# A two-block hybrid layer stack: first block's projections moved ahead, as block products through DRAM

## The chip, the cores and the metric

One Trainium2 chip, one core. The metric is device microseconds (us) from the start to the end of one execution, the median of several runs.

## What is computed

Two transformer-like blocks follow each other on 1024 tokens of width 1024; only the first is changed. It puts 16 learned tokens in front (1040 in all), normalises, and multiplies by one wide matrix `w_in`. The columns of that product feed two mixers, whose gated outputs are summed, projected and added to the input.

```python
u = rmsnorm(h, norm_pre);  proj = u @ w_in
z_ssd, xbc, dt_raw, z_att, q, k, v, f_raw, g_raw = split(proj)
# SSD mixer: 32 heads of 64 channels in 4 groups, chunks of 128 tokens
xs, bm, cm = split(silu(causal_depthwise_conv(xbc)))
dt = softplus(dt_raw + dt_bias);  a_cs = cumsum(dt * a)          # inside a chunk
decay = exp(where(causal, a_cs[l] - a_cs[s], -inf))
y = (C B^T * decay) @ (xs*dt)  +  exp(a_cs) * (C @ h_in)         # h_in: state carried from chunk to chunk
y_ssd = gated_group_rmsnorm(y + d_skip * xs, z_ssd)
# forgetting attention: 16 heads of 64, causal
logit[t, s] = q_t . k_s / 8 + sum_{s<j<=t} log sigmoid(f_j)
y_att = (softmax(logit) @ v) * silu(z_att)
merged = sigmoid(g) * (y_ssd @ w_proj_ssd), sigmoid(g') * (y_att @ w_proj_att), added
x1 = h + rmsnorm(merged @ w_out)
```

The second block (differential and dilated attention, gated embedding) follows on `x1`.

## The kernel before

Everything is channel-major, in strips of 128 channels by all tokens. A projection of a strip (`project`) is a sum over eight row blocks of the input; each float32 product is done as three matmuls of rounded parts (`mm3`, lines 111 to 114: high with high, low with high, high with low), over pieces of at most 512 tokens, one PSUM bank each. The weights of a strip come by DMA on SP's queue, ScalarE (ACT) makes the high part, GpSimd (POOL) subtracts for the low part (`split_sb`, lines 117 to 121). The first block has 88 strips: 48 are needed for 1024 tokens (q, the gates za, zs and g) and 40 for 1040 (k, v and the 24 of the convolution's input `xbc`).

The order of work is written out by hand: generators yield after each piece with an estimate of TensorE's time, and `merge` interleaves two of them in a given ratio. Each engine runs its instructions in the order in which this code emits them.

- Attention goes head pair by head pair (eight), `fox_attend`: for each of eight query tiles, stage A makes the scores (lines 566 to 569), on VectorE (DVE) the sum with the forget gates and a running minimum (line 570), the exponential on ACT (line 573) and a small copy on POOL (line 576); stage B transposes (line 620) and evacuates (line 626); stage C multiplies by v (line 599). While a pair's tiles run, the projections of the next pair stand between them.
- The SSD goes group by group (four): first the group's six strips are projected and convolved (`ssd_project`), then eight chunks run (`ssd_chunks`), with the eight strips of zs and g between their steps. A chunk's step prepares the next one (`prep`: decayed exponentials on lines 714 to 722) and then does its own products (lines 747 and 750) and sums.

```python
            nx = {}
            if p < 7:
                merge(att, self.fox_project(p + 1, nx), 2.5, lead=2000.0)
...
            side = chain(z, zipped(self.gates(ms), rows))
            merge(self.ssd_chunks(g, st), side, 2.0 if g < 3 else 1.7)
```

Projected strips stay in SBUF until they are used; only the mixers' outputs and the gates go to DRAM. Then `merge_out` multiplies by the two output matrices, and the second block begins.

Of the kernel before, what the change touches and what calls it, by code (L numbers as in the profile page):

```python
# [22 lines left out]
SLOT = 1044  # L23
EPS = 1e-6
# [42 lines left out]
class Kern:  # L67
    def __init__(self, ctx, tc, t, out):
        self.tc, self.nc, self.t, self.out = tc, tc.nc, t, out
        self.big = ctx.enter_context(tc.tile_pool(name="big", bufs=41))  # L70
# [6 lines left out]
        self.halfs = None  # L77

# [5 lines left out]
    def half(self, name):  # L84
        """512 columns; in the tail from a pool of their own"""
# [4 lines left out]
    def psum(self, one, two):  # L90
        """the banks of PSUM from here on: single ones and pairs"""
# [40 lines left out]
    # weight strips, in the order in which they are used  # L132
# [63 lines left out]
    def consts(self):  # L196
# [16 lines left out]
        V.tensor_scalar(out=self.gbh, in0=self.pslot("gate_bias"), scalar1=0.5, scalar2=None, op0=ALU.mult)  # L213
        self.sb48 = cst.tile([48, 1], F32, name="sb48")
        V.tensor_tensor(out=self.sb48, in0=self.pslot("b48")[:48], in1=self.pslot("sgn")[:48], op=ALU.mult)

# [1 line left out]
    def rstd(self, out, ss, n):  # L218
        """1 / sqrt(ss / n + eps)"""
# [9 lines left out]
    def rsqrt(self, v, pool):  # L229
        """v [128, n] > 0 in place to 1/sqrt(v): a first guess from the exponent, three Newton steps"""  # L230
# [29 lines left out]
    def token_sums_T(self, t, n):  # L260
        """the sums by tokens: [128 tokens, block of 128, part, 32]"""
# [5 lines left out]
    def rows_out(self, v, n, dst):  # L267
        """v [128 tokens, n = (row, block of 128)]: rows of 1024 tokens in DRAM"""
# [22 lines left out]

    def prologue(self):
        nc, t = self.nc, self.t
        self.uh = [self.slot(f"uh{k}", F32R) for k in range(KD)]
        self.ul = [self.slot(f"ul{k}", F32R) for k in range(KD)]
        rows = [t["meta_tokens"]] + [t["x"][i * 128:(i + 1) * 128] for i in range(8)]
        ss = self.cst.tile([128, 9], F32, name="ss0")
        xs = []
        for i, r in enumerate(rows):
            p = r.shape[0]  # L300
            x = self.slot("x", w=D)
            nc.sync.dma_start(out=x[:p], in_=r)
            xs.append(x)
            if i == 0:
                self.const_loads()
            if i == 2:
                self._wload(0)
                self._wload(1)
        gain = self.pslot("norm_pre")
        for g, c0 in (((0, 1, 2), 0), ((3, 4, 5), 272), ((6, 7, 8), 656)):  # L310
            for i in g:
                p = rows[i].shape[0]
                j = self.slot("junk", w=D)
                nc.scalar.activation(out=j[:p], in_=xs[i][:p], func=AF.Square, accum_out=ss[:p, i:i + 1])
                self.rstd(ss[:p, i:i + 1], ss[:p, i:i + 1], D)
                nc.vector.tensor_scalar(out=xs[i][:p], in0=xs[i][:p], scalar1=ss[:p, i:i + 1], scalar2=None,
                                        op0=ALU.mult)
            yield
            if c0 == 0:
                self.consts()  # L320
            self.normed_T([xs[i][:rows[i].shape[0]] for i in g], gain, self.u1, c0)
            yield

# [1 line left out]
    def softplus(self, x):  # L325
        """x [128, 9, n] in place to max(x, 0) + log(1 + exp(-|x|)), the logarithm by the series of artanh"""
# [16 lines left out]
    def dt_f(self):  # L343
        nc, cst = self.nc, self.cst
        raw = self.slot("dtf")
        sgn = self.pslot("sgn")

        def consume(ps, c0, c1):
            nc.scalar.activation(out=raw[:48, c0:c1], in_=ps, func=AF.Identity, scale=sgn[:48], bias=self.sb48)

        yield from self.project("w48", self.u1, PIECES_P, consume, m=48)
# [10 lines left out]
        V = nc.vector  # L362
        self.softplus(sp[:, :, 32:48])
        yield 3000
        # cumulative log forget gates (negated: csp), as rows
# [27 lines left out]
        nc.sync.dma_start(out=self.d_csp, in_=row[:16, :L])  # L393
        self.softplus(sp[:, :, 0:32])
# [1407 lines left out]
```

## Time and profile before

| | |
|---|---|
| median of three runs | 2735.22 us (2734.06 to 2739.91) |
| the profiled execution's own span | 2737.4 us |
| busy: TensorE (PE), DVE, ACT, POOL | 2670.8, 1377.0, 1171.9, 685.0 us |
| granted TensorE clock, mean | 0.994 |
| first block, up to the first matmul of `merge_out` | 0 to 1421 us |
| attention's pairs | 79 to about 682 us |
| SSD's groups | about 660 to 1401 us |
| `merge_out`, w_out and the second block | 1421 to 2737 us |

The profile gives no separate run time for the profiled execution; its span lies 2.2 us (0.08%) above the median. "Busy" is the time in which an engine has an instruction under way; matmuls overlap each other, so TensorE's pace is read from the distance between starts and not from the duration of one.

### The profile page before, as it was taken

The page shows a single profiled execution, that of the slowest core. Times are in us where ns is not written, and L with a number is a line of the kernel's source. Part 1 is how long each engine was busy: PE and PEld are TensorE (multiplying, and loading weights), DVE is VectorE, ACT ScalarE, POOL GpSimd, SP SyncE. Part 2 cuts the span into 40 slices and gives each one's busy share as a digit, 9 for nine tenths or more (in the row PEclk, how much of TensorE's full clock was granted, in tenths as well). Part 3 has the DMA queues.
Part 4 walks back from the last instruction along what each step waited for, and adds up shares of the span by engine and source line. Part 5 has one row for each costly group of instructions (what it writes and reads, how often), then busy time and mean ns, then how long its engine had stood idle before and what let it go on. Part 6 is the DMA issues. An engine that isn't in the chain of part 4 may idle for free. (4 is left out here: it accounts for less than half of the span.)

```text
span 2737.4 us, 40266 instructions
## 1 busy us (share of the span) xinstructions
PE 2670.8 (98%) x15693; PEld 2264.5 (83%) x15693; DVE 1377.0 (50%) x2761; ACT 1171.9 (43%) x2080; POOL 685.0 (25%) x764
## 2 busy tenths in 40 slices
PE   8999999999999999999999999999999999998999
PEld 6888888889989989889887887877878877787887
DVE  5433222333474574664756777445644555446332
ACT  5444444454343443434432113445544554445331
POOL 1111111111244243342433334111111121114321
PEclk9999999999999999999999999999999999999999
DMA  3212222211123123122157654340222223324422
GB/s 124 65 57 78 71 78 78 78 47 47 70 83 118 47 85 116 49 84 108 62 186 253 215 185 161 108 130 26 85 62 78 79 79 97 98 72 138 166 67 70
DMA packets 85471, 266.98 MB, mean 98 GB/s; under 512 B 10880, under 2 KB 12032, under 8 KB 84256
## 3 DMA queue, kind: packets, MB, share of 16 engines
q1 hardware_dynamic: 85280, 264.40, 29.9%
q8 instruction: 123, 2.02, 0.3%
q14 instruction: 68, 0.56, 0.1%
HBM read 205.57 MB, written 33.49 MB: 87 GB/s over the span
## 5 line engine op out<-in xcount | busy, mean ns | idle before, releaser
L121 POOL TENSOR_TENSOR wlo<-wraw,whi 128x1024 fp32r<-128x1024 f32 (+2 forms) x168 | 374.3, 2231 | 1279.5 <-ACT whi L120 1242.6
L112 PE MATMUL bank<-uh,whi 128*128 128x512 f32 (+4 forms) x1752 | 628.4, 359 | 0.1
L114 PE MATMUL bank<-uh,wlo 128*128 128x512 f32 (+4 forms) x1752 | 619.7, 354 | 0.4 <-POOL wlo L121 0.4
L113 PE MATMUL bank<-ul,whi 128*128 128x512 f32 (+4 forms) x1752 | 619.5, 354 | 0.0
L112 PEld LDWEIGHTS bank<-uh,whi 128*128 128x128 f32 (+1 forms) x1752 | 328.9, 188 | 36.4 <-issue 3.5
L114 PEld LDWEIGHTS bank<-uh,wlo 128*128 128x128 f32 (+1 forms) x1752 | 328.6, 188 | 35.9 <-POOL wlo L121 0.9
L113 PEld LDWEIGHTS bank<-ul,whi 128*128 128x128 f32 (+1 forms) x1752 | 328.9, 188 | 32.2
L112 PE MATMUL bank<-u,whi 128*128 128x512 f32 x512 | 207.6, 405 | 0.7 <-ACT pr L931 0.7
L113 PE MATMUL bank<-u,whi 128*128 128x512 f32 x512 | 203.5, 397 | 0.0
L114 PE MATMUL bank<-u,wlo 128*128 128x512 f32 x512 | 203.2, 397 | 0.0
L120 ACT ACTIVATE whi<-wraw 128x1024 fp32r<-128x1024 f32 (+2 forms) x169 | 155.6, 927 | 24.3 <-DMA wraw<-in_w_pa_dram 15.1
L626 ACT ACTIVATE pt<-bank 128x512 f32<-128x512 f32 (+1 forms) x320 | 143.4, 507 | 37.2 <-PE bank L620 28.0
L114 PE MATMUL bank<-yh,wlo 128*128 128x512 f32 x384 | 153.0, 399 | 2.0 <-POOL wlo L121 1.9
L112 PE MATMUL bank<-yh,whi 128*128 128x512 f32 x384 | 152.8, 398 | 1.0 <-ACT whi L120 1.0
L113 PE MATMUL bank<-yl,whi 128*128 128x512 f32 x384 | 152.1, 396 | 0.0
L643 DVE SCALAR_TENSOR_TENSOR acc<-raw,cwh,acc 128x1040 f32<-128x1040 f32 x72 | 93.7, 1302 | 114.0 <-ACT acc L640 112.3
L573 ACT ACTIVATE N<-N,mn 128x272 f32<-128x272 f32 (+7 forms) x128 | 100.6, 786 | 54.3 <-DVE mn L570 51.8
L114 PEld LDWEIGHTS bank<-u,wlo 128*128 128x128 f32 x512 | 97.3, 190 | 23.0
L112 PEld LDWEIGHTS bank<-u,whi 128*128 128x128 f32 x512 | 97.6, 191 | 22.1 <-ACT pr L931 1.1
L113 PEld LDWEIGHTS bank<-u,whi 128*128 128x128 f32 x512 | 97.6, 191 | 20.6
L121 POOL TENSOR_TENSOR wo<-wl,wo 128x512 fp32r<-128x512 f32 x52 | 75.1, 1456 | 156.8 <-ACT wo L120 116.5
L620 PE MATMUL bank<-cm,N 128*128 128x128 f32 x832 | 108.2, 275 | 0.0
(326 smaller groups left out, 4997.5 us busy)
## 6 DMA issues: line engine op xcount, KB each, us to landing
wraw<-in_w_in_dram SPq DMA_DIRECT2D x120, 512.0 KB, 4.6
gt<-d_gate SPq DMA_DIRECT2D x48, 512.0 KB, 4.8
ab<-d_acs SPq DMA_DIRECT2D x32, 512.0 KB, 3.6
qs<-qt SPq DMA_DIRECT2D x48, 256.0 KB, 3.0
wl<-in_w_out_dram SPq DMA_DIRECT2D x48, 256.0 KB, 4.1
tab<-in_tab_dram SPq DMA_DIRECT2D x8, 1056.0 KB, 5.6
cb<-d_csp SPq DMA_DIRECT2D x16, 520.0 KB, 6.1
d_gate<-gt SPq DMA_DIRECT2D x16, 512.0 KB, 2.9
```

Source lines behind the costliest of these rows:

```text
L112: te.matmul(ps, lh, rh, start=start, stop=False)
L113: te.matmul(ps, lh, rl, start=False, stop=False)
L114: te.matmul(ps, ll, rh, start=False, stop=stop)
L120: self.nc.scalar.activation(out=hi, in_=src, func=AF.Copy)
L121: (self.nc.vector if vector else self.nc.gpsimd).tensor_tensor(out=lo, in0=src, in1=hi.bitcast(F32), op=ALU.subtract)
L573: nc.scalar.activation(out=N[:, :W], in_=N[:, :W], func=AF.Exp, scale=-1.0, bias=mn[:, n - 1:n], accum_out=self.lall[:, 2 * p + j, i:i + 1])
L620: nc.tensor.transpose(ps[:, b * 128:(b + 1) * 128], N[:, c:c + 128], self.ident)
L626: self.nc.scalar.activation(out=out, in_=ps, func=AF.Copy)
L643: V.scalar_tensor_tensor(out=acc[:, :L], in0=raw[:, k:k + L], scalar=w(k), in1=acc[:, :L], op0=ALU.mult, op1=ALU.add)
```

## The change

Nothing is changed in the second block. In the first:

1. All projections run first, in one stage (`dense`). Two strips make a pair with a 2x2 block structure (output strip by half of the input channels), the tokens are halved (528 columns each for 1040 tokens, with 16 in both; 512 for 1024), and the eight block products of four row blocks become seven, by sums of blocks ahead and behind (`FACTORS`). The sums of the input's blocks are made once in `prologue`. For each pair POOL makes four sums of weight blocks and six of the seven low parts, DVE the seventh, and DVE adds each product out of PSUM. There are 24 pairs of the short kind (one matmul of 512 columns per block) and 20 of the long (two of 264).
2. All results go to DRAM: q and k already split, v by tokens, the convolved xbc, the gates' functions.
3. Then a second stage has attention (all 64 tiles as one stream) and the SSD (36 steps as one stream: for each group, the 16 tokens in front and eight chunks) alone, interleaved by `merge` with ratio 0.5. Their operands are loaded back from DRAM, 13 loads a head pair, four a chunk.
4. In a chunk, the eight subtractions on DVE before one exponential of 1024 columns become a mask addition of 1024 columns on POOL and eight exponentials of 128 columns with a bias on ACT; the d_skip product moves to POOL; the state is one plain float32 product and not three of parts; gate and squares are done in the chunk. Two query tiles share a product with v.

```diff
+    FACTORS = (("A11", "B11"), ("S2", "T2"), ("A12", "B21"), ("S3", "T3"), ("S1", "T1"), ("A22", "T4"), ("S4", "B22"))
...
+    def product(self, i, f, subs, banks):
+        d = self.hl.pop((i, self.FACTORS[f][0]))
+        T = self.TB[self.FACTORS[f][1]]
+        for (a, b), ps in zip(subs, banks):
+            for k in range(4):
+                c = slice(k * 128, k * 128 + 128)
+                self.mm3(ps[:, :b - a], d[:, 0, c], d[:, 1, c], T[k][:, 0, a:b], T[k][:, 1, a:b], k == 0, k == 3)
...
+            d = self.hl[i, n] = self.ph.tile([128, 2, 512], F32R, tag="hl", name="hl", bufs=6)
+            nc.scalar.activation(out=d[:, 0], in_=x, func=AF.Copy)
+            (V if n == "S4" else G).tensor_tensor(out=d[:, 1], in0=x, in1=d[:, 0].bitcast(F32), op=ALU.subtract)
...
+                G.tensor_tensor(out=r8(ab), in0=r8(ab), in1=self.nmask.unsqueeze(1).to_broadcast([128, 8, 128]),
+                                op=ALU.add)
+                for k in range(8):
+                    nc.scalar.activation(out=ab[:, k * 128:(k + 1) * 128], in_=ab[:, k * 128:(k + 1) * 128], func=AF.Exp,
+                                         bias=self.nacs[:, c, 8 * g + k:8 * g + k + 1])
+                V.tensor_tensor(out=r8(ab), in0=r8(ab), in1=ps[:, :128].unsqueeze(1).to_broadcast([128, 8, 128]),
+                                op=ALU.mult)
...
+                V.tensor_tensor(out=th, in0=E[:, :512], in1=yh, op=ALU.mult)
+                V.tensor_tensor(out=y, in0=xD, in1=yp, op=ALU.add)
+                yp = yh = None
+                G.tensor_tensor(out=y, in0=y, in1=th, op=ALU.add)
...
+                V.scalar_tensor_tensor(out=r8(y), in0=r8(y), scalar=0.5, in1=z, op0=ALU.mult, op1=ALU.mult)
+                nc.sync.dma_start(out=self.d_yssd[4 * g:4 * g + 4, :, 128 * c:128 * c + 128].rearrange("q p l -> p q l"),
+                                  in_=r8(y))
+                nc.scalar.activation(out=th, in_=y, func=AF.Square)
+                G.tensor_tensor(out=th[:, :256], in0=th[:, :256], in1=th[:, 256:], op=ALU.add)
+                G.tensor_tensor(out=acc[:, 128 * c:128 * c + 128], in0=th[:, :128], in1=th[:, 128:256], op=ALU.add)
...
+        self.dense(pairs, 2, chain(self.prologue(), self.dt_f(), self.dt_ssd()))
+        del self.TB
+        MARK("fox_ssd")
+        self.pools(32)
+        merge(self.fox_attend(), self.ssd_all(), 0.5)
+        acc, self.last_acc = self.last_acc, None
+        run(self.ssd_ssq(3, {"acc": acc}))
+        del acc
+        self.pools(41)
```

**Place 1, TensorE in a chunk's step.** Before, in the third chunk of the first group: L114 with `uh` is the end of one piece of a projection; L747 and L750 are the chunk's products, L112 to L114 with `xdd` its state, L671 to L708 the next chunk's transposes and its C B^T, and L112 with `uh0` begins the next piece of 24 matmuls of 512 columns.

```order
L114 MATMUL bank_7617<-uh7_8_95,wlo_561_7411 128x512
L747 MATMUL bank_7644<-ab_563_7478,xdt_7485 64x128 x8
L750 MATMUL bank_7645<-acc_527_6911,h_7476 128x128 x4
L112 MATMUL bank_7668<-xdd_7492,bt_7489 128x512
L113 MATMUL bank_7668<-xdd_7492,bt_7489 128x512
L114 MATMUL bank_7668<-xdd_7492,bt_7489 128x512
L671 MATMUL bank_7677<-cm_107,acc_532_7004 128x128
L678 MATMUL bank_7684<-cm_107,acc_522_6796 128x128
L708 MATMUL bank_7692<-acc_527_6911,acc_522_6796 128x128
L112 MATMUL bank_7719<-uh0_1_88,whi_567_7545 128x512
```

The same place of the changed kernel, in the second group: L1050 to L1066 prepare the next chunk, L949 and L1000 are transposes of attention's stage B, L1106 to L1117 the chunk's products and state, L931 and L932 the scores of the next query tile.

```order
L1050 MATMUL bank_11839<-cm_98,x_11665 128x128 x4
L1057 MATMUL bank_11846<-cm_98,bc_11666 128x128
L1066 MATMUL bank_11852<-bc_11666 128x128
L949 MATMUL bank_11870<-cm_98,pm_11435 128x128
L1000 MATMUL bank_11891<-cm_98,N_356_11646 128x128 x4
L1106 MATMUL bank_11897<-ab_11568,xdt_11678 64x128 x8
L1109 MATMUL bank_11898<-bc_11565,h_11663 128x128 x4
L1117 MATMUL bank_11916<-xdd_11684,bt_11682 128x512
L931 MATMUL bank_11926<-kx_337_11378,qs_336_11377 128x400
L932 MATMUL bank_11926<-ky_338_11379,qs_336_11377 128x400
```

No projection stands between a chunk's parts any more; attention's tiles stand there.

**Place 2, DVE in the same step of the changed kernel.** L1052 and L1078 belong to the preparation of the next chunk (L1078 multiplies the exponentials `ab` by C B^T), L950 and L1008 evacuate attention's transposes, L1111 to L1129 are the chunk's own sums, L935 and L981 attention's next scores and its output.

```order
L1052 TENSOR_TENSOR xdt_11844<-bank_11839,dtx_765 128x512
L1078 TENSOR_TENSOR ab_11669<-ab_11669,bank_11852 128x1024
L950 COPY pm_11435<-bank_11870 128x128
L1008 COPY pt_11788<-bank_11891 128x4x128
L1111 TENSOR_TENSOR th_11911<-E_11688,bank_11898 128x512
L1112 TENSOR_TENSOR y_11912<-xD_11702,bank_11897 128x512
L1122 TENSOR_TENSOR h_11829<-h_11829,bank_11916 128x512
L1129 SCALAR_TENSOR_TENSOR y_11912<-y_11912,z_11570 128x512
L935 ISA N_363_11924,mn_11925<-cb_339_11384,bank_11926 128x400
L981 SCALAR_TENSOR_TENSOR y_329_11203<-bank_11772,zs_317_10915 128x512
```

Everything on DVE behind L1078, attention's evacuations among it, now stands behind a product whose input comes through POOL and ACT.

**Place 3, POOL from one step to the next.** Before, in the same stage: L740 carries the state, L684 decays x, L757 adds, L121 is the low part of a projection's weights.

```order
L740 TENSOR_TENSOR h<-h,E 128x512
L684 TENSOR_TENSOR xr_7493<-xdt,dec 128x512
L757 TENSOR_TENSOR yq_7351<-yq_7351,th_7529 128x128
L757 TENSOR_TENSOR yq_7352<-yq_7352,th_7529 128x128
L121 TENSOR_TENSOR wlo_7546<-wraw_7414,whi_7545 128x1024
```

In the changed kernel: L941 is the small copy of attention's stage A (one per head and tile), L1096 carries the state, L1061 decays x, L1073 adds the mask, L1081 multiplies by d_skip, L1114 adds the two parts of the output, L1133 and L1134 add squares.

```order
L941 COPY pm_11753<-N_362_11820 128x16
L1096 TENSOR_TENSOR h_11829<-h_11663,E_11688 128x512
L1061 TENSOR_TENSOR xdd_11850<-xdt_11844,dec_978 128x512
L1073 TENSOR_TENSOR ab_11669<-ab_11669,nmask_171 128x1024
L1081 TENSOR_TENSOR xD_11868<-x_11665,params_100 128x512
L1114 TENSOR_TENSOR y_11912<-y_11912,th_11911 128x512
L1133 TENSOR_TENSOR th_11911<-th_11911 128x256
L1134 TENSOR_TENSOR acc_357_11746<-th_11911 128x128
L941 COPY pm_11753<-N_363_11924 128x16
L941 COPY pm_11753<-N_376_11996 128x16
L1096 TENSOR_TENSOR h_12022<-h_11829,E_11854 128x512
```

The mask addition, the d_skip product and the squares are new on POOL, and attention's copies stand ahead of each step. Counted along POOL's whole order, 5 of the 64 tiles stand ahead of the first chunk's step, 42 stand in the steps of 19 chunks, 17 stand with no chunk's work beside them (where a group's sum of squares is taken), and the last 13 chunks stand behind the last tile.

## Rows read from the trace of the kernel before

**Rows 1.** Stretches of the span: busy us (count) by engine, PEclk, DMA share, GB/s.
```profile
75.00:660.00 585.00, 583.65 (x4200) 515.85 (x4199) 189.73 (x582) 277.52 (x609) 106.65 (x220) 1.00 0.23 68
660.00:1421.00 761.00, 760.59 (x4504) 667.07 (x4503) 434.62 (x825) 301.21 (x466) 272.50 (x250) 1.00 0.24 85
```

**Rows 2.** TensorE's groups, shapes apart: name, shape, count | busy us, mean ns | idle before.
```profile
L112 PE MATMUL bank<-uh,whi 128*128 128x512 f32 x768 | 307.8, 401 | 0.0
L747 PE MATMUL bank<-ab,xdt 128*64 128x128 f32 x512 | 35.0, 279 | 0.0
L750 PE MATMUL bank<-acc,h 128*128 128x128 f32 x256 | 37.1, 288 | 0.0
```

**Rows 3.** Timeline of TensorE, 350 and 2290 us: start us, duration us, line.
```profile
350.04 0.32 PE L112 MATMUL bank<-uh,whi 128*128 128x348 f32 x1
...
352.43 0.33 PE L112 MATMUL bank<-uh,whi 128*128 128x348 f32 x1
...
2290.02 0.40 PE L114 MATMUL bank<-u,wlo 128*128 128x512 f32 x1
...
2294.89 0.39 PE L114 MATMUL bank<-u,wlo 128*128 128x512 f32 x1
```

**Rows 4.** Timeline of all engines, 795 to 810 us, a chunk's step.
```profile
795.65 2.26 DVE L718 TENSOR_SCALAR ab<-ab,acs 128x128 f32<-128x128 f32 x8
799.10 1.23 DVE L722 TENSOR_TENSOR ab<-ab,cbm 128x1024 f32<-128x1024 f32 x1 [1.19 <-ACT ab L721]
804.86 4.17 DVE L718 TENSOR_SCALAR ab<-ab,acs 128x128 f32<-128x128 f32 x8
...
798.00 1.06 ACT L721 ACTIVATE ab<-ab 128x1024 f32<-128x1024 f32 x1 [2.39 <-DVE ab L718]
...
803.53 2.43 POOL L121 TENSOR_TENSOR wlo<-wraw,whi 128x1024 fp32r<-128x1024 f32 x1
```

**Rows 5.** POOL's groups, shapes apart.
```profile
L121 POOL TENSOR_TENSOR wlo<-wraw,whi 128x512 fp32r<-128x512 f32 x48 | 81.2, 1704 | 177.5 <-ACT whi L120 151.5 <-PE bank L114 14.6 <-DMA wraw<-in_w_ps_dram 4.9
L740 POOL TENSOR_TENSOR h<-h,E 128x512 f32<-128x512 f32 x28 | 29.5, 1052 | 0.0
L576 POOL COPY pm<-N 128x16 f32<-128x16 f32 x128 | 25.3, 198 | 287.1 <-ACT N L573 286.0
L782 POOL TENSOR_TENSOR zq<-zq,zq 128x1024 f32<-128x1024 f32 x6 | 14.4, 2404 | 29.3 <-ACT zq L780 29.0
```

**Rows 6.** ACT's groups, the first with its shapes together, the others apart.
```profile
L573 ACT ACTIVATE N<-N,mn 128x272 f32<-128x272 f32 (+7 forms) x128 | 100.6, 786 | 54.3 <-DVE mn L570 51.8 <-issue 1.2 <-DVE raw L635 0.6
L714 ACT ACTIVATE E<-ab 64x512 f32<-64x512 f32 x64 | 40.1, 626 | 25.5 <-DMA ab<-d_acs 13.5 <-DVE th L752 11.6
L680 ACT ACTIVATE bt<-bank 128x128 fp32r<-128x128 f32 x28 | 7.6, 273 | 6.5 <-PE bank L678 6.3
```

**Rows 7.** DVE's groups, shapes together.
```profile
L570 DVE CUSTOM_DVE_ANT_0 N<-cb,bank 128x272 f32<-128x272 f32 (+7 forms) x128 | 60.3, 490 | 79.1 <-PE bank L569 59.9 <-PE bank L567 16.7 <-ACT N L573 2.1
L570 DVE CUSTOM_DVE_ANT_0 N<-cb,bank,mn 128x348 f32<-128x348 f32 (+4 forms) x96 | 56.1, 584 | 14.6 <-PE bank L567 1.0
L722 DVE TENSOR_TENSOR ab<-ab,cbm 128x1024 f32<-128x1024 f32 x32 | 39.2, 1226 | 37.9 <-ACT ab L721 37.9
L752 DVE TENSOR_TENSOR th<-E,bank 128x512 f32<-128x512 f32 x32 | 21.8, 681 | 10.7 <-PE bank L750 10.7
```

**Rows 8.** The page's bytes moved, by fortieths of the span.
```profile
GB/s 124 65 57 78 71 78 78 78 47 47 70 83 118 47 85 116 49 84 108 62 186 253 215 185 161 108 130 26 85 62 78 79 79 97 98 72 138 166 67 70
```

**Rows 9.** TensorE's timeline from 2298 us, then the stretch 2301 to 2306 us.
```profile
2298.11 0.42 PE L1262 MATMUL bank<-qs,qs 128*128 128x400 f32 x1 [1.96 <-DMA qs<-qt]
2300.38 0.67 PE L1262 MATMUL bank<-qs,qs 128*128 128x400 f32 x1 [1.39 <-DMA qs<-qt]
2302.09 0.63 PE L113 MATMUL bank<-u,whi 128*128 128x512 f32 x1
2301.00:2306.00 5.00, 5.00 (x15) 4.07 (x14) 1.10 (x4) 2.01 (x5) 3.32 (x11) 0.50 0.26 105
```

More of the change, by code (lines that the diff above doesn't have):

```diff
@@ L23 @@
 SLOT = 1044
+H = 528
 EPS = 1e-6
@@ L310, in prologue @@
[L310 to L317, printed above, removed]
-            yield
-            if c0 == 0:
-                self.consts()
-            self.normed_T([xs[i][:rows[i].shape[0]] for i in g], gain, self.u1, c0)
+        xs = [None] * 9
@@ new lines, in transposed @@
+        def transposed(ids, k):
+            ps = self.bank()
+            w = 0
+            for i in ids:
+                r = rows[i].shape[0]
+                nc.tensor.transpose(ps[:, w:w + r], xs[i][:r, k * 128:(k + 1) * 128], self.ident[:r, :r])
+                w += r
+            return ps[:, :w]
+        load(0)
+        self.const_loads()
+        gain = self.pslot("norm_pre")
+        for i in range(1, 5):
+            load(i)
+        yield
+        for i in range(5, 9):
+            load(i)
@@ new lines, in dense, with start @@
+    def dense(self, pairs, early, side):
+        names = [a for a, _ in self.FACTORS]
+        first, rest = ["A11", "A12"], [a for a in names if a not in ("A11", "A12")]
+        order = [(i, n) for i in range(early) for n in first] + [(i, n) for i in range(early) for n in rest]
+        order += [(i, n) for i in range(early, len(pairs)) for n in names]
+        fac, done, count = self.factors(pairs, order), 0, 0
+        outs = [[] for _ in pairs]
+        gens = {}
+        post = iter(())
+        def start(i):
+            kind, _, _, f = pairs[i]
+            gens[i] = self.pair(i, kind == "L", 3 if f == self.post_xbc else 0, outs[i], i < early)
+        next(side)
+        next(fac)
+        done = 1
+        next(side)
+        for i, _ in order:
+            if i not in gens:
+                start(i)
+            count += 1
+            while done < min(len(order), count + 5):
+                next(fac)
+                done += 1
+            next(gens[i])
+            next(post, None)
+            next(side, None)
+            if (i, names[-1]) == order[count - 1]:
+                run(post)
+                run(gens.pop(i))
+                post = pairs[i][3](pairs[i][1][0], pairs[i][2][0], outs[i])
+        run(post)
+        run(side)
@@ L614, in transposes @@
+        yield from self.inv_rows(16, self.d_rl)
+    def transposes(self, N, off, nb, pts, act=False):
         nc = self.nc
@@ L727, in ssd_chunks @@
-        _, xdd, bt = tokens(0, 0, 16)
-        xdd = split(xdd, 16)
-        nx = prep(0)
-        yield 1700
-        ps = state(bt, xdd, 16)
-        h = self.ph.tile([128, 512], F32, tag="h", name="h", bufs=2)
-        nc.scalar.activation(out=h, in_=ps, func=AF.Copy)
-        yield 1000
-        for c in range(8):
-            cols = slice(16 + 128 * c, 144 + 128 * c)
-            ab, E, xdt, xdd, bt = nx
-            if c < 7:
-                hn = self.ph.tile([128, 512], F32, tag="h", name="h", bufs=2)
+                            in1=self.sp[:w, c + 1, hs].unsqueeze(2).to_broadcast([w, 8, 64]), op=ALU.mult)
@@ L759, in ssd_chunks @@
-            if c < 7:
-                ps = state(bt, xdd, 128)
-                V.tensor_tensor(out=hn, in0=hn, in1=ps, op=ALU.add)
-                h = hn
-            yield 1800
-    def ssd_z(self, g, st):
-        st["zs"] = []
-        for q in range(4):
-            zs = self.slot("zq", w=T)
-            st["zs"].append(zs)
-            yield from self.project(("zs", 4 * g + q), self.u1, PIECES_T,
-                                    lambda ps, c0, c1: self.silu2(ps, zs[:, c0 - 16:c1 - 16]))
@@ L773, in ssd_gate @@
[L773 to L787 removed]
+            load(n + 2)
@@ new lines, in build @@
+        xbc = []
+        for g in range(4):
+            for j, k in ((16 + g, 20 + g), (4 * g, 4 * g + 1), (4 * g + 2, 4 * g + 3)):
+                xbc.append(("L", (("xbc", j), W1[16 + j]), (("xbc", k), W1[16 + k]), self.post_xbc))
+        light = gate[2:] + qza + zs
+        heavy = xbc + kv
+        pairs = gate[:2]
+        while light or heavy:
+            pairs += light[:1] + heavy[:1]
+            del light[:1], heavy[:1]
+        self.dense(pairs, 2, chain(self.prologue(), self.dt_f(), self.dt_ssd()))
```

725 lines of the change are left out of this document (463 added, 262 removed).

## The prediction

> **What bounds the kernel now.** I read the page's busy shares first: TensorE has something under way for 2670.8 of 2737.4 us, the others for half the span or less. The stretches say where: in the first block TensorE is busy for 583.65 of 585 us while attention runs, and for 760.59 of 761 us while the SSD runs; DVE is busy for 190 and 435 us there, POOL for 107 and 273 [rows 1]. So every wait of the two mixers is covered by projection matmuls, and the first block lasts as long as its matmuls do. The reader is to keep two things apart: how much matmul work there is, and whether something is always ready to be multiplied.
>
> How dense is it? The groups give a mean of 401 ns for a matmul of 512 columns [rows 2], but these overlap; starts are 0.1593 us apart for 348 columns (15 steps from 350.04 to 352.43) and 0.2319 for 512 (21 steps from 2290.02 to 2294.89) [rows 3]. A straight line between the two gives 0.122 for 264 columns.
>
> **The dense stage.** Before, 48 strips take 48 x 2 x 24 = 2,304 matmuls of 512 columns, 534 us, and 40 strips 40 x 3 x 24 = 2,880 of 344 to 348 (all but a few), 459 us: 993 us. The 768 on one of `mm3`'s three lines [rows 2] fit. Afterwards 24 short pairs have 7 x 4 x 3 = 84 matmuls of 512 each, 2,016, 468 us, and 20 long pairs 168 of 264, 3,360, 410 us: 878 us. That takes off **115 us**, an eighth less the 16 columns that both halves hold. The small product for dt and f grows from 72 to 120 matmuls, 4 us back.
>
> Is this stage still TensorE's? A short and a long pair take 84 x 0.232 + 168 x 0.122 = 40 us. POOL has 20 operations of 512 columns for them: 20 x 1.70 = 34 us at the dearest row of such a subtraction, 21 at the cheapest operation of that size [rows 5]. DVE adds 7 x 0.68 for the short and about as much for the long, two low parts, and the convolution's eight operations of some 1.3, about 25. Both fit, with weights five products ahead. So I take 40, and keep 20 x 2 us for the case that POOL runs over.
>
> The start costs more: the first product needs five rows of the input and not three, normalised and transposed in 16 pieces of about 0.6 on ACT and DVE, so I put it at 22 us. Before the second kind of product, 20 block sums are split in two on ACT, DVE and POOL, some 6 us for each of four row blocks, with four early products (11 us) and part of dt under it: 12 us of idling. With 30 us of transposes and dt, the stage ends near 22 + 878 + 15 + 30 + 12, about **960 us**.
>
> **The two streams.** What is left for them is 1421 - 960 = 461 us for a tie, less the seams. Their matmul work is what the first block had besides: 1409 busy us less 993, and less about 55 (an estimate) for dt, the transposes into u and v by tokens, 361 us. A chunk has 3.6 of them: (35.0 + 37.1)/32 for its products [rows 2], the rest for transposes and state at the pace of rows 3. If TensorE stayed busy, the change would win 80 us. But the projections that filled the waits are gone (place 1), so I follow the chunk's chain.
>
> In the kernel before, a step already shows how strictly an engine keeps its order. At 795.65 DVE's eight subtractions run for 2.26 us, ACT takes the exponential at 798.00, DVE waits 1.19 for it and multiplies at 799.10; ACT had waited 2.39 [rows 4]. From one engine to the next it takes 0.04 to 0.09 us. Nothing behind a waiting instruction passes it.
>
> Now the changed step (places 2 and 3), alone, from the moment POOL is free. State 1.05 and decay 1.05 (the row of 512 [rows 5]); mask addition of 1024, 2.40 by the same rows (between 2.1, twice the 512, and 2.43 [rows 4]); eight exponentials of 128 on ACT, 2.2 at 0.273 each [rows 6]; DVE's product of 1024, 1.23; its two sums of 512 that stand behind it, 1.36 [rows 7]; POOL's addition 1.05; DVE's gate 0.68; ACT's square 0.63 [rows 6]; POOL's additions of 256 and 128, some 0.6 and 0.4 between the rows of 16 and 512. Only then comes POOL's next state. The sum is 12.65, with eight hand-overs **13 us**. POOL is at work for 7.6 of them, TensorE for 3.6.
>
> A query tile costs, one head after the other: minimum 0.91 on DVE ((60.3 + 56.1)/128) [rows 7], twice; the second exponential, 0.79, with its read-out about 1 [rows 6]; POOL's two copies at 0.2 [rows 5]; and two to three evacuations of up to 0.6, which stand in front of the next step's exponentials. About 3.2 us. Could it run in the 5 us in which DVE waits for the exponentials? By place 2 it can't: the tile's evacuations and minima stand behind the product, and the tiles emitted after a chunk's sums are awaited by POOL's copies ahead of the next state (place 3). About 1.5 us of a step's first tile run beside the square and the additions. So a step with 2.2 tiles (42 in 19) takes 13 + 2.2 x 3.2 - 1.5 = 18.5 us.
>
> The sum of the stage, by the counts below place 3: start, 5 MB for the first pair and the first chunks behind them at no more than 253 GB/s [rows 8], 20 us, and five tiles, 16 us; 19 steps of 18.5, 352 us; 17 tiles without a chunk, at TensorE's own 3.8 each (361 less 32 x 3.6, over 64), 65 us; 13 chunks alone, 169 us; four pieces of 16 tokens and the sums of squares, 22 us. That is 644 us, TensorE busy for 361.
>
> **The clock.** Before, two idle spells of 1.96 and 1.39 us between 2296 and 2300 are followed by matmuls of 512 columns with 0.63 us and not 0.40, at a granted 0.50, that is 1.2 GHz, from 2301 to 2306 [rows 9]. A step of 18.5 us with 12 us of matmuls, several of its idle spells longer than those, will see that level. Part of TensorE's work stands on the path (the products with v before DVE's output every fourth tile, the scores before the minima). I add 40 us, between 0 and 361, which would be all of the two streams' matmuls at half pace with nothing to hide it: near the low end, since in 13 steps alone and most of the rest TensorE waits anyway. The stage is then **684 us**. The Trainium skill, "TensorE: Matmul & The Clock Gate" (What's actually happening), says that a gate sets one of these two levels by how busy the array has recently been; the trace agrees, with 0.50 after the two spells. With full pace throughout the sum would be 40 us less; by that rule, taken for the whole stage, it would be the rival of the slow clock below.
>
> **The sum.** Second block and merge 2737.4 - 1421 = 1316; dense stage 960; two streams 684; the last chunk's sum of squares and the first loads of the merge, which nothing covers any more, 15. Together **2975 us** against the profile's 2737.4, which lies 0.08% above the median 2735.22.
>
> **The rivals.**
> *The streams hide each other.* TensorE has both streams' work in its queue, and POOL, DVE and ACT have about 270, 330 and 340 us each. If the steps with tiles take what their matmuls take (361 less 13 x 3.6 is 314) and the 13 steps alone take POOL's 7.6 (99), the stage is 433 with its start: 1316 + 960 + 433 + 15 = 2724; with the tail hidden too 2650. It decides for faster when the stage stays below about 445. For it speaks that each stage of attention stands two tiles ahead; against it the order of places 2 and 3.
> *Half hidden.* If about half of a tile runs beside the chain and POOL's operations are at their cheap end, a step takes 14 and a chunk alone 12: 36 + 266 + 65 + 156 + 22 + 20 for the clock is 565, and the time 2856.
> *The slow clock rules.* If the gate stays at 1.2 GHz through the stage, its 361 us become 722, and with start and tail (some 60 us of idling on top) it takes about 780: 3070.
> *The dense stage is POOL's.* The products then don't save what they should: 20 x 2 us more and 3015, or, with DVE held as well, the saving of 115 gone altogether. In rows 4 the subtractions on DVE take 4.17 us and not 2.26 where POOL works. The Trainium skill, "SBUF — State Buffer" (SBUF: two separate sides), has it that the two share a port pair, which one of them holds for a whole instruction; the trace agrees there.
>
> **How the numbers follow.** Chances: forecast 0.57 (2880 to 3060 by itself), half hidden 0.20, hidden 0.13, slow clock 0.06, POOL's dense stage 0.04. The range 2740 to 3060 leaves out the hidden case and the slow clock. Faster by over 0.2% (about what a measurement here can tell from nothing) 0.14: the hidden case and a little of its neighbour; within 0.2% 0.02; slower 0.84.
>
> **What would show it.** Of the profile after: TensorE busy without gaps up to about 960 us, with starts of 264 columns near 0.122 apart; then its share falls to 50 to 60% for some 680 us, the clock below 1 in that stretch; DVE idle before the product of 1024 by ACT's exponentials for 4 us or more a step, ACT idle before them by POOL's mask addition; 13 us from step to step at the end, without any tile. Wrong it would be if steps with two tiles take 14 us or less, if TensorE stays over 80% there, or if the dense stage ends past 1000.

## The result, and the profile after

The changed kernel takes 3049.89 us (median of four runs, 3046.89 to 3051.74), the kernel before in the same job 2734.93 us (2734.06 to 2739.91): 1.1145 times as long, 95% interval 1.1129 to 1.1161. The forecast was 2975, slower, in a range of 2740 to 3060. The profiled execution's span is 3049.6 us.

The page of after, its busy times and its fortieths (76 us each):

```profile
PE 2673.2 (88%) x15389; PEld 2222.4 (73%) x15389; DVE 1557.9 (51%) x2788; ACT 1236.4 (41%) x2329; POOL 1256.2 (41%) x1191
...
PE   3699999999999577778755499999999999998999
...
PEclk8899999999999688889776699999999999999999
```

TensorE is busy for as long as before (2670.8), though it has some 115 us of matmuls less: in the first block about 215 us of its busy time now fall into stretches at the lower clock, which stretches them. The same by stages (columns as in [rows 1]): the dense stage, its seam, the two streams with tiles, the chunks alone, the second seam, and the merge with the second block.

```profile
0.00:1008.00 1008.00, 931.18 (x5704) 833.93 (x5704) 541.56 (x747) 366.70 (x589) 691.72 (x565) 0.97 0.33 107
1008.00:1021.00 13.00, 0.42 (x3) 0.14 (x1) 3.05 (x3) 2.00 (x2) 0.00 (x0) 0.60 0.54 193
1021.00:1521.00 500.00, 374.03 (x2495) 285.83 (x2496) 236.32 (x675) 251.20 (x638) 173.57 (x258) 0.83 0.51 154
1521.00:1706.00 185.00, 99.07 (x544) 69.98 (x542) 62.75 (x102) 64.38 (x174) 96.12 (x90) 0.70 0.33 94
1706.00:1735.00 29.00, 2.41 (x8) 0.74 (x8) 11.20 (x21) 5.67 (x8) 0.19 (x1) 0.51 0.73 205
1735.00:3049.00 1314.00, 1266.10 (x6640) 1031.82 (x6640) 703.07 (x1242) 546.40 (x920) 294.62 (x278) 0.99 0.36 114
```

The first block now ends at 1735 and not at 1421, and the rest is as long as it was (1314.6 us against 1316.6). So all of the loss lies in the first block, and most of it in stretches in which no engine is near full: in the 500 us with tiles TensorE has 75%, DVE 47%, ACT 50%, POOL 35%, DMA 51%.

TensorE's timeline in the dense stage answers to [rows 3]: starts of 512 columns stand 0.23 us apart as before, those of 264 columns 0.122 (15 steps between these two rows).

```profile
701.07 0.29 PE L122 MATMUL bank<-B,hl 128*128 128x264 f32 x1
...
702.90 0.29 PE L122 MATMUL bank<-B,hl 128*128 128x264 f32 x1
```

Its pauses stand at the stage's two ends (in brackets the idle time before the row and what ended it); ahead of dt's two sums there are two more, of 6.71 and 6.35 us:

```profile
31.63 0.78 PE L122 MATMUL bank<-B,hl 128*128 128x512 f32 x1
46.33 0.45 PE L336 MATMUL bank<-cm,xrow 128*128 128x128 f32 x1 [7.69 <-DVE xrow L329]
89.07 0.46 PE L122 MATMUL bank<-B,w48s 128*48 128x264 f32 x1 [30.42 <-ACT w48s L130]
1020.89 0.46 PE L931 MATMUL bank<-kx,qs 128*128 128x144 f32 x1 [12.58 <-DMA kx<-d_k]
1734.99 0.80 PE L122 MATMUL bank<-yh,whi 128*128 128x512 f32 x1 [23.03 <-DMA wraw<-in_w_pa_dram]
```

In the second stage the timeline of all engines, 1651 to 1666 us, shows one chunk alone, from one mask addition (L1073) to the next:

```profile
1651.82 2.34 POOL L1073 TENSOR_TENSOR ab<-ab,nmask 128x1024 f32<-128x1024 f32 x1
1654.19 2.44 ACT L1076 ACTIVATE ab<-ab,nacs 128x128 f32<-128x128 f32 x8 [4.12 <-POOL ab L1073]
1656.72 1.22 DVE L1078 TENSOR_TENSOR ab<-ab,bank 128x1024 f32<-128x1024 f32 x1 [8.26 <-issue]
...
1658.46 0.68 DVE L1112 TENSOR_TENSOR y<-xD,bank 128x512 f32<-128x512 f32 x1
1659.22 1.27 POOL L1114 TENSOR_TENSOR y<-y,th 128x512 f32<-128x512 f32 x1 [4.06 <-DVE y L1112]
1660.52 0.69 DVE L1129 SCALAR_TENSOR_TENSOR y<-y,z 128x512 f32<-128x512 f32 x1 [0.78 <-POOL y L1114]
1661.25 0.63 ACT L1132 ACTIVATE th<-y 128x512 f32<-128x512 f32 x1 [4.61 <-DVE y L1129]
1661.95 0.72 POOL L1133 TENSOR_TENSOR th<-th 128x256 f32<-128x256 f32 x1 [1.47 <-ACT th L1132]
1662.75 0.46 POOL L1134 TENSOR_TENSOR acc<-th 128x128 f32<-128x128 f32 x1
1663.16 1.04 POOL L1096 TENSOR_TENSOR h<-h,E 128x512 f32<-128x512 f32 x1
...
1665.16 2.35 POOL L1073 TENSOR_TENSOR ab<-ab,nmask 128x1024 f32<-128x1024 f32 x1
```

That is the forecast's chain, link by link, each waiting for the one above it, in 13.34 us (left out are the first of DVE's two sums, 0.68, and POOL's decay, 1.05). And in a step with two tiles, the timeline of DVE:

```profile
1288.40 1.22 DVE L1078 TENSOR_TENSOR ab<-ab,bank 128x1024 f32<-128x1024 f32 x1 [7.32 <-ACT ab L1076]
...
1289.74 0.68 DVE L1008 COPY pt<-bank 128x512 f32<-128x512 f32 x1
```

and that of POOL:

```profile
1295.95 0.45 POOL L1134 TENSOR_TENSOR acc<-th 128x128 f32<-128x128 f32 x1
...
1301.52 0.20 POOL L941 COPY pm<-N 128x16 f32<-128x16 f32 x1 [4.84 <-ACT N L938]
1302.51 0.20 POOL L941 COPY pm<-N 128x16 f32<-128x16 f32 x1 [0.80 <-ACT N L938]
1302.67 1.04 POOL L1096 TENSOR_TENSOR h<-h,E 128x512 f32<-128x512 f32 x1
```

POOL has finished the chunk at 1296.4 and could carry the next state, but copies of 0.2 us (L941) stand ahead and wait for the tile's exponential until 1302.5. Attention's evacuations on DVE stand behind a product that waited 7.32 us. The chain of the tile and that of the chunk are run one behind the other.

### The profile page after: what moved, and what is told of

It reads as the page before. It is cut to its first block, busy times and chain, and to the rows that moved or that the text cites. A ratio compares the mean times of both kernels' runs of the same rounds, so it can differ in the third digit from the quotient of the medians.

```text
span 3049.6 us, 41430 instructions
## 1 busy us (share of the span) xinstructions
PE 2673.2 (88%) x15389; PEld 2222.4 (73%) x15389; DVE 1557.9 (51%) x2788; ACT 1236.4 (41%) x2329; POOL 1256.2 (41%) x1191
## 5 line engine op out<-in xcount | busy, mean ns | idle before, releaser
L131 POOL TENSOR_TENSOR wlo<-wraw,whi 128x512 fp32r<-128x512 f32 (+1 forms) x80 | 157.8, 1982 | 745.0 <-ACT whi L130 727.6
L122 PE MATMUL bank<-T,hl 128*128 128x264 f32 (+1 forms) x1024 | 335.9, 328 | 0.0
L124 PE MATMUL bank<-T,hl 128*128 128x264 f32 (+1 forms) x1024 | 334.3, 326 | 0.0
L123 PE MATMUL bank<-T,hl 128*128 128x264 f32 (+1 forms) x1024 | 333.5, 326 | 0.0
L443 POOL TENSOR_TENSOR hl<-raw,hl 128x512 fp32r<-128x512 f32 x132 | 207.3, 1571 | 174.0 <-ACT hl L442 170.9
L442 ACT ACTIVATE hl<-S 128x512 fp32r<-128x512 f32 x176 | 107.4, 628 | 397.2 <-POOL S L422 383.3
L122 PE MATMUL bank<-B,hl 128*128 128x264 f32 (+1 forms) x768 | 251.0, 327 | 0.0
L124 PE MATMUL bank<-B,hl 128*128 128x264 f32 (+1 forms) x768 | 250.8, 327 | 0.0
L123 PE MATMUL bank<-B,hl 128*128 128x264 f32 (+1 forms) x768 | 249.3, 325 | 0.0
L443 POOL TENSOR_TENSOR hl<-S,hl 128x512 fp32r<-128x512 f32 x132 | 187.8, 1435 | 110.2 <-ACT hl L442 110.2
L124 PEld LDWEIGHTS bank<-T,hl 128*128 128x128 f32 x1024 | 192.9, 188 | 17.4
L123 PEld LDWEIGHTS bank<-T,hl 128*128 128x128 f32 x1024 | 193.3, 189 | 16.1
L122 PEld LDWEIGHTS bank<-T,hl 128*128 128x128 f32 x1024 | 193.2, 189 | 15.0
L479 DVE TENSOR_TENSOR o<-u,bank 128x264 f32<-128x264 f32 (+2 forms) x192 | 99.1, 519 | 144.0 <-PE bank L124 143.9
L123 PEld LDWEIGHTS bank<-B,hl 128*128 128x128 f32 x768 | 145.1, 189 | 12.5
L124 PEld LDWEIGHTS bank<-B,hl 128*128 128x128 f32 x768 | 145.0, 189 | 12.5
L122 PEld LDWEIGHTS bank<-B,hl 128*128 128x128 f32 x768 | 145.2, 189 | 11.6
L1078 DVE TENSOR_TENSOR ab<-ab,bank 128x1024 f32<-128x1024 f32 x32 | 39.1, 1221 | 223.7 <-ACT ab L1076 111.5
```

The costliest lines, as they stand in the source:

```text
L122: te.matmul(ps, lh, rh, start=start, stop=False)
L123: te.matmul(ps, lh, rl, start=False, stop=False)
L124: te.matmul(ps, ll, rh, start=False, stop=stop)
L131: (self.nc.vector if vector else self.nc.gpsimd).tensor_tensor(out=lo, in0=src, in1=hi.bitcast(F32), op=ALU.subtract)
L442: nc.scalar.activation(out=d[:, 0], in_=x, func=AF.Copy)
L443: (V if n == "S4" else G).tensor_tensor(out=d[:, 1], in0=x, in1=d[:, 0].bitcast(F32), op=ALU.subtract)
```

## The experiments

Eleven kernels were run, once each, beside 2733.5 to 2738.2 us of the kernel before; the four runs of after differ by 5 us, so a difference of that size is not read as an effect. A chunk's step is read from the starts of its last addition of squares on POOL. These rows give their count, the shortest, median and longest in ns, and the first and last start in us. In after these are five steps with two to three tiles, 20.7 us each, and five alone, 13.4:

```profile
L1134 POOL TENSOR_TENSOR acc<-th x6: 453/457/463, 1071.3 to 1174.8; 128x128 f32<-128x128 f32 x6
L1134 POOL TENSOR_TENSOR acc<-th x6: 452/453/455, 1622.7 to 1689.5; 128x128 f32<-128x128 f32 x6
```

"The stage" is the time from the first scores to the last chunk's last addition, 685 us in after.

**1. Are the two streams one chain?** First the ratio of `merge`, so that no chunks are left over at the end; then each stream by itself.

```diff
-        merge(self.fox_attend(), self.ssd_all(), 0.5)
+        merge(self.fox_attend(), self.ssd_all(), 0.8)   # e1_ratio
+        merge(self.fox_attend(), self.ssd_all(), 0.0)   # e11_one_by_one
```

> The two streams are interleaved at 0.8 and not 0.5, so that the 13 chunks at the end get tiles beside them. Theory (the order chain: a chunk costs 13.3 us from POOL to POOL and a tile about 3.2 more, whoever stands where): only the 1.5 us that a step's first tile hides are won, at most 13 x 1.5 = 20 us: 3030, between 3015 and 3050. Rival (imbalance: TensorE idles in the 13 steps alone, and tiles would fill that): 13 x (13.3 - 3.6) = 126 us less, 2925.

> The merge's ratio 0: all of attention's 64 tiles first, then all chunks, neither beside the other. Theory (in the kernel after nothing of a tile is hidden in a chunk's step: 20.5 us with two tiles is 13.3 + 2 x 3.7, where the two steps over a group's end give (69.9 - 28.3)/11 and (65.7 - 28.3)/10, 3.8 and 3.7 us for a tile alone): attention 16 + 64 x 3.8 = 260, chunks 32 x 13.3 and four group starts, 485, together 745 and not 698, so 3085 to 3110, only 1 to 2% over the kernel after. Rival (the two streams do hide some of each other, and a tile alone takes its chain of minimum, exponential and transposes, 7 us or more): attention 450, together 930, 3250 or more.

With 0.8 it took 3032.7 us (stage 664): the uneven end was worth 17 us, as the theory had it, and not the rival's 126. One after the other took 3107.2 us, inside its theory's 3085 to 3110, the stage 737 us, attention 271 of them (4.2 a tile) and the chunks the rest, in steps of 13.35 (four from 1337.6 to 1391.0). Its stretches, attention and then the chunks:

```profile
1020.00:1300.00 280.00, 244.12 (x1875) 198.69 (x1876) 151.97 (x540) 161.22 (x379) 25.13 (x128) 0.96 0.54 169
1300.00:1740.00 440.00, 220.51 (x1134) 152.97 (x1133) 141.27 (x227) 149.68 (x419) 233.94 (x209) 0.66 0.38 105
```

So interleaving hides 52 us of 737, and it is the chunks that leave TensorE idle: attention alone keeps it busy for 87% of its time, they for 50%.

**2. Which links hold the chunk?** The mask addition went to DVE, whose product of 1024 takes 1.22 where POOL's takes 2.34; and the product was emitted behind the chunk's own sums, so that these don't wait for it; then both with the ratio 0.8.

```diff
-                G.tensor_tensor(out=r8(ab), in0=r8(ab), in1=self.nmask.unsqueeze(1)...   # e2_mask_dve, e7
+                V.tensor_tensor(out=r8(ab), in0=r8(ab), in1=self.nmask.unsqueeze(1)...
...
-                V.tensor_tensor(out=r8(ab), in0=r8(ab), in1=ps[:, :128]...               # e3_late_product, e7
...
+            nx = scored(nx)      # that product, at the end of the chunk's step
```

> The mask addition of 1024 columns runs on DVE and not on POOL. Theory (order chain): it can start when ACT's first exponentials are done, 1.7 us earlier, and takes about 1.2 and not 2.34: 2.8 us less in each of 32 steps, 90 us, 2960; a step alone 10.5. Rival (tiles and TensorE's lower clock bound the steps that have tiles): only the 13 steps alone win, 36 us, 3014. Rival (DVE is the scarce engine): no gain, or slower by 32 x 1.2.

> DVE's product of the exponentials with C B^T is emitted behind the chunk's own sums and not ahead of them; nothing else. Theory (order chain): DVE's sums no longer wait for ACT's exponentials, so a step alone is POOL's 9.3 us and not 13.3: 52 us in 13 steps and about as much each in the 19 others, 2920, at least 2960. Rival (the exponentials' latency is needed anyway, the place on DVE doesn't matter): 3050, unchanged.

> The late product, the mask addition on DVE and the ratio 0.8 together. Each alone took 62, 34 and 4 us off (2975.3, 3003.4, 3032.7 against 3049.9 and, in the same job, some 3037 by their own sums). Theory (three separate pieces of one chain, which add): a chunk alone 7 to 9 us, the stage 540 to 570, 2905 to 2935. Rival (in the steps with tiles the chain through TensorE and attention is the longer one, so only the chunks alone win): 2945 to 2975.

e2 took 3003.4 us, e3 2975.3, e7 2939.2 (stages 640, 610, 568). The steps of e3, with tiles and alone:

```profile
L1139 POOL TENSOR_TENSOR acc<-th x7: 455/457/461, 1068.0 to 1179.5; 128x128 f32<-128x128 f32 x7
L1139 POOL TENSOR_TENSOR acc<-th x5: 453/457/457, 1577.7 to 1614.7; 128x128 f32<-128x128 f32 x5
```

Alone a step falls to 9.25 us, in e2 to 11.1 (four from 1600.6 to 1644.9), as the chain says. With tiles it falls only to 18.6 (the same six take 20.4 in after), in e2 to 19.6 (five from 1068.1 to 1166.0): there the chunk's links are not the whole. Both expectations of the larger gain were missed. Against after's 3049.9 the three single edits took 75, 47 and 17 us off (the 62, 34 and 4 of e7's expectation count from some 3037 that no run shows), 139 together; e7 took 111 off and came out between its theory and its rival. What else makes the steps with tiles long is looked for in the tile's part.

**3. Is it attention's copies on POOL?** Twice their place was changed: emitted two tiles later, in stage B right ahead of their transpose (e4), and one tile later with attention's output on DVE (L981) put off as well (e8).

```diff
-                nc.gpsimd.tensor_copy(out=M[t // 4][:, 0, c:c + 16], in_=N[:, 0:16])             # in stage A of tile t
+                nc.gpsimd.tensor_copy(out=M[t // 4][:, 0, c:c + 16], in_=Ns[t][j][:, 0:16])      # e4: in stage B of t; e8: in stage A of t + 1
```

> POOL's two small copies of a tile are emitted two tiles later, with the tile's transposes, so that POOL no longer waits for that tile's exponentials ahead of a step. Theory (order chain): in the 19 steps with tiles the state and the decay start 1 to 2 us earlier, 20 to 40 us in all, 3020; steps alone stay at 13.3. Rival (ACT's queue or DVE's is what the step waits for, POOL's wait is beside it): under 10 us, 3045.

> Only attention's part of the slots: a tile's copies on POOL are emitted at the start of the next tile, and attention's output on DVE at the start of the tile behind it; the chunks as in the kernel after. Theory (a step with tiles is long because POOL waits for attention's exponential ahead of the chunk's next state, 202 us of waits, and DVE for attention's sums, 24): the steps with two tiles fall by 2 to 4 us, 17 steps, 2990 to 3015. Rival (these waits only move behind another instruction, as with the copies two tiles later): 3035 to 3065.

e4 took 3079.5 us, 30 more, which neither of its expectations had; e8 took 3040.0, as its rival said. The largest of the waits of after (1040 to 1520 us), and two smaller ones: who waits for whom, us in total, times, longest.

```profile
POOL pm L941 <- ACT N L938: 202.3, 110, 7.9
...
POOL y L1114 <- DVE y L1112: 43.3, 16, 5.6
...
POOL xdd L1061 <- DVE xdt L1052: 26.4, 10, 6.3
```

Those of e4 (1040 to 1550):

```profile
POOL xdd L1062 <- DVE xdt L1053: 115.5, 18, 12.8
POOL y L1115 <- DVE y L1113: 97.0, 18, 8.8
...
POOL pm L947 <- ACT N L938: 56.9, 22, 8.0
...
PE bank L950 <- POOL pm L947: 53.1, 11, 10.3
```

In e4 the wait that was the largest sum, 202 us, shrinks to 57, and nothing is won: POOL waits for the chunk's own parts in its place (115 and 97 us, where it was 26 and 43), and TensorE for the copy, 53 us, since the copy now stands behind the chunk's work on POOL. A sum of waits on one engine is no price. That theory fell. Nor do the loads from DRAM hold this stage in after: of its waits in these 480 us, those that the profile puts down to a DMA come to some 10 us.

**4. Is it the clock?** e5 puts 60 products of the identity on TensorE ahead of each chunk's products.

```diff
+                fb = self.bank()
+                for _ in range(FILL):       # 60
+                    te.matmul(fb[:, :128], self.identb, self.identb)
```

> 60 products of the identity (128 columns, into a bank that nothing reads) stand on TensorE ahead of each chunk's own products: 32 x 60, at some 0.06 us each (a quarter of 0.232) 3.6 us a chunk at full pace, 115 us in all. They change no output and use time in which TensorE waits for DVE's product. Theory (the chain of the engines sets the step, the clock only where TensorE's work stands on it): the chunks alone stay at 13.3 us, the granted clock below 1 falls from 256 us to under 120, and the steps with tiles change by no more than a microsecond; 3030 to 3060. Rival A (the low clock is what makes a step with two tiles 20 us and not 17): those steps get 2 us shorter or more, 3010 or less. Rival B (TensorE has no time over in the steps with tiles): the steps get longer by most of the 3.6 us, 3100.

It took 3074.7 us. A stretch with chunks alone in after:

```profile
1629.00:1699.00 70.00, 32.10 (x174) 23.88 (x174) 24.54 (x34) 23.76 (x68) 38.43 (x35) 0.67 0.31 87
```

and in e5:

```profile
1650.00:1720.00 70.00, 44.02 (x499) 37.03 (x497) 24.53 (x34) 23.31 (x66) 38.88 (x35) 0.89 0.32 87
```

Granted 0.89 and not 0.67, a chunk alone takes the same 13.35 us (four from 1656.6 to 1710.0): there the clock costs nothing. With tiles the steps got 1.2 us longer (five of 21.9 from 1074.4 to 1183.8), though over the whole stage the granted clock rose from 0.80 to 0.88 (276 us below full pace in after, 174 in e5). The total lies between the theory's 3060 and rival B's 3100; rival A's 3010 or less did not come. But with tiles this decides little: the 60 products hold TensorE for 3.5 us a step themselves, and a gain of some 2 us a step from the clock could hide behind them. A bound comes from after: in the 500 us with tiles TensorE is busy for 123 us while the lower level is granted, so full pace would shorten its own work there by 62 us at most. What the clock costs between nothing and that stays open.

**5. Is it the order altogether?** In e6 a chunk's preparation is cut into six pieces that stand between the chunk's own sums, each a slot behind what it needs, with tiles between the slots; attention is as in e8. The ratio of `merge` is set anew for these slots, so that tiles last almost to the end of the stage, and the sums of squares at a group's end leave room for 4 tiles and not for 11. e9 adds four things: a pair's loads in three parts, the sums of squares in slots, w48's split ahead of the T blocks, the merge's first weights earlier. e10 is e9 with the mask on DVE.

```diff
-                nx = prep(n + 1)
-            yield 900
+                nx = p1(n + 1)           # transposes, xdt, E
+            yield 100
+            f[0](nx)                     # p2: decay, mask (POOL)
...
+                yield 100                # behind the chunk's products
...
+                f[1](nx)                 # p3: skip term; then output, state; p4: exponentials; p5: cb; p6: product
...
-        merge(self.fox_attend(), self.ssd_all(), 0.5)
+        merge(self.fox_attend(), self.ssd_all(), 0.117)
...
-                sts[p + 1] = self.fox_load(p + 1)                     # e9: at tiles 1, 3 and 5
+                    self.fox_load_qk(p + 1, sts[p + 1], 0)
```

> The same arithmetic in another order of emission: a chunk's preparation is cut into six pieces that stand between the chunk's own sums (state and decay; mask; skip term; exponentials; cb; product), each a slot after what it needs, with tiles between the slots; a tile's copies on POOL and attention's output on DVE are emitted one tile later. Theory (the loss is the order of instructions within each engine, and the work itself would fit): a step comes to some 11 to 13 us with two tiles, and the stage to 360 to 450 us and not 685; 2730 to 2815. Rival A (each slot still waits for the slot ahead through another engine, as the late copies did): 15 us a step, stage 520, 2885. Rival B (the engines slow one another when they work at once, so that the order doesn't matter): the stage stays over 600, 2960 or more.

> The slots as before (2891.5), and four things more: a pair's eleven loads are issued in three parts over the tiles of the pair before, and not in one block ahead of the next chunk's loads; the sums of squares and the 16 tokens of the next group stand in slots too; w48 is split ahead of the sums of the T blocks; the merge's first weights are loaded and split ahead of its inputs. Theory (with the order mended, the 58 us in which TensorE waits for the load of x, up to 14 us each behind a pair's 4 MB, are what is left over the work): stage 440 to 470 and not 526; the merge starts 5 us sooner after the last chunk; dense stage 6 to 12 us shorter if its 30 us are DVE's work on the T blocks, 25 or more if they are the place of w48's split. Together 2795 to 2825. Rival (the loads only cover waits between the engines): stage 490 or more, 2840 to 2865.

> The same with the mask addition on DVE and not on POOL. Theory (a step is still a chain through POOL, DVE and ACT, of which DVE's 1.2 us for 1024 columns is the shorter link than POOL's 2.4): 10 to 30 us below the run with the loads spread. Rival (each engine is by now held by its own work in order, and DVE has the more): from 5 us below to 15 above it.

e6 took 2891.5 us (stage 526), e9 2817.5 (471), e10 2822.3 (480). The stage in e6:

```profile
1020.00:1546.00 526.00, 409.63 (x3038) 312.54 (x3038) 297.55 (x776) 310.58 (x811) 268.97 (x348) 0.91 0.59 179
```

the wait in it that e9 was made for:

```profile
PE bank L1072 <- DMA x<-d_xbc: 58.5, 8, 14.0
```

the same wait in e9 (1010 to 1460):

```profile
PE bank L1096 <- DMA x<-d_xbc: 10.5, 5, 3.9
```

and e9's dense stage and its second:

```profile
0.00:991.00 991.00, 931.33 (x5704) 832.91 (x5704) 542.70 (x748) 366.65 (x589) 692.18 (x565) 0.98 0.34 109
1004.00:1475.00 471.00, 400.18 (x3025) 308.33 (x3026) 299.96 (x774) 309.38 (x810) 269.45 (x348) 0.94 0.67 198
```

With the same instructions on the same engines, in another order, the stage goes from 685 to 526 and 471 us, and TensorE's busy share from 69% to 85%. Neither e6's first theory (360 to 450) nor its rival B (over 600) held; the 526 is rival A's 520, but its 15 us a step is not what the steps show: the 28 inside the groups take 12.9 on average, near the theory's 11 to 13, and the rest stood where the groups change (45, 42 and 37 us) and where x was late. How much of e6's 158 us is the slots and how much the new spread of the tiles was not tried apart; in the old order the ratio alone was worth 17 (e1) and attention's later copies and output 10 (e8). e9 came out as its theory said (2795 to 2825). The 55 us of its stage come from the spread loads and the sums in slots together, which were not tried apart either. At the last seam it wins 14 us, but its merge and second block take 11 more than e6's (1323.7 and 1312.5). With the mask on DVE nothing is won any more: rival right.

No version beats the kernel before. e9 is the nearest, 3% over it.

## Why the prediction was right in sign and 75 us short

- **Second block and merge**: 1316 forecast, 1314.6 measured.
- **Dense stage**: 960 forecast, 1008.3. By the forecast's own sign (past 1000) this part of it was wrong. Its matmuls came as worked out (878 forecast, 881 by the distances of their starts), and POOL, busy for 692 of 1008 us, didn't bind: behind 156 us TensorE has no gap of more than 0.3 us. Three small terms were mis-sized: the first product at 31.6 and not 22 us; 30.4 us of waiting ahead of dt and not 12; and 22.9 us for the second half of the input, dt and its sums (7.69, 6.71, 6.35 and one of 2.1), which the sum had as work and not as waits. Together 51, of which the stage shows 48, as the rest took 42 and not its 15 + 30 (the text doesn't derive the 15). The T blocks' sums take 9.52 us a row block (62.56 to 72.08 on DVE) and not 6; DVE's subtractions take twice as long there while POOL works (last section). In e9, with only w48's split moved in this stage, it ended 17.6 us sooner: so much of the 30 was the split's place in ACT's order, and the rest stayed.
- **A chunk alone**: 13 forecast, 13.3 measured, and each link as placed; POOL's addition (1.27) and the exponentials (2.44) were a little dearer. e2 and e3 confirm it: they shorten it by the links that they take out.
- **A step with tiles**: 18.5 forecast, 20.0 measured (16 steps, 320 us); why it is 1.5 longer is not shown. **Tiles alone** 3.8 forecast, 4.2 in e11.
- **The clock's 40 us**: it was granted low, as forecast (0.83 and 0.70), but as a price it is not borne out: zero where chunks are alone, and not known with tiles. The stage, from the dense stage's end, took 698 and not 684, and without the 40 the sum was 644: the missing 54 are mostly the steps with tiles (16 x 1.5), the group changes (136 us for two, with 21 tiles, against 117 by the forecast's numbers, 21 x 3.8 + 2 x 13 + 11) and the start (9). So the term had the right size, but no run shows the clock as its cause, and that the sum came so near owes something to luck.
- **Last seam**: 15 forecast, 28.8 measured: after the sum of squares the merge's inputs and weights are loaded and split one after another.

48, 14 and 14 less 1 are the 75 us.

Of the other signs that it named, the chunk's 13 us, the waits of DVE and ACT in it, and starts 0.122 apart came; TensorE's share of the second stage was to be 50 to 60% and is 69%.

Of the rivals, "the streams hide each other" fails in this order, but e9 shows that its reason (the engines have time enough) was right in the main: counted from the dense stage's end, as the forecast counts, its stage takes 484 us, against the 445 from which that rival decides. It still would not win. In e9 TensorE idles 60 us in the dense stage, 71 in the second and 30 in two seams, some 160 in all, where in the first block before it idled 15 (1406.2 busy of 1421). Its busy time falls by only some 72 us of the 115 that the seven products save, since part of what is left runs at the lower clock; so its first block is 71 us longer than before. "The slow clock rules" needs the lower level through the whole stage; it was granted for 276 of 685 us, and cost nothing where chunks are alone. "The dense stage is POOL's" is excluded by its 69% and by TensorE's gapless run.

The Trainium skill, "Perfetto Trace Analysis" (Roofline), says that a kernel with low use of both matmul and memory is bound by latency, that is by stalls and dependencies. The trace agrees in the second stage, as far as numbers go (the section sets no bound for low): the matmuls in it, 361 us at full pace by the forecast's estimate, are 53% of the 685 us, DMA is busy for 46%, and a new order of the same instructions takes 214 us off (685 to 471).

What stays open: how the 20 us of a step with tiles divide between the tile's chain on ACT and DVE and the waits for banks on TensorE; how much a low clock costs there; and which part of the new order wins most. A kernel that keeps the block products and still has projections between the two streams was not run.

## What to carry to other kernels

Work that seems to cost an engine time (projections here) may be what hides two latency-bound chains; before it is moved away or shrunk, add up what those chains take alone, link by link, from durations. That the work of two streams fits on in-order engines doesn't make them hide each other. Here it took a new order on every engine at once: each instruction about one slot behind what it waits for, loads in pieces, the tiles spread evenly; moving the one instruction with the largest wait only moved the wait. A chain added up link by link gave the length of a chunk's step alone to within 3% here, that of a step with tiles to within 8%.

## What the runs showed of the hardware

- Raising TensorE's granted clock from 0.67 to 0.89 with idle products changed a step bound by other engines by nothing (13.36 and 13.35 us).
- In after, DVE's float32 subtraction of 528 columns takes 0.71 us almost by itself and 1.57 on average (two in 3.14) while POOL subtracts; the rows of DVE:

```profile
56.91 0.71 DVE L389 TENSOR_TENSOR T<-t,T 128x528 fp32r<-128x528 f32 x1
57.98 3.14 DVE L389 TENSOR_TENSOR T<-t,T 128x528 fp32r<-128x528 f32 x2 [0.36 <-ACT T L388]
```

and of POOL at the same time:

```profile
57.49 1.34 POOL L389 TENSOR_TENSOR B<-x,B 128x528 fp32r<-128x528 f32 x1 [2.66 <-ACT B L388]
58.78 1.77 POOL L389 TENSOR_TENSOR T<-t,T 128x528 fp32r<-128x528 f32 x1
```

- A load of 256 KB issued on SP's queue behind a pair's 13 loads (5424 KB in one block) came so late that TensorE stood for up to 14.0 us (e6); with the 13 issued in three parts the longest such wait was 3.9 (e9).
